# v split into hi and lo where it is projected, gated rows turned and split where they are made, and q read from PSUM in residue order

## The chip, the core and the metric

The kernel runs on one core of one Trainium2 chip. The metric is the device time of one execution in microseconds. A core has a matrix engine (PE, with its weight loads PEld), three engines that compute on tiles (DVE, ACT, POOL) and the engine SP, which here issues every DMA. Each engine runs its own instructions in order and waits on semaphores for the others. Tiles lie in SBUF (on-chip memory, 128 partitions); PE writes into PSUM, which has 8 banks of 128 x 512 float32.

## What is computed

One decoder layer on 1024 tokens of width 1024, all in float32. Cut to the part that the change touches:

```
a = rmsnorm(x);  q, k, v, u, z = split(a @ w_in)          # each 1024 x 512
attn = dilated_attention(q, k, v)                          # 8 heads of 64; windows with dilation 1, 4, 16
sgu  = gelu(u) * (w_spatial_causal @ layernorm(gelu(z)) + b_spatial)      # chunks of 128 tokens
mixed = concat(rmsnorm(attn), rmsnorm(sgu)) @ w_out
h = x + rmsnorm(mixed)
h = h + rmsnorm((silu(g) * up) @ w_down)                   # g, up = rmsnorm(h) @ w_gate_up
out = h + sigmoid(h @ w_pe_gate + b) * (p @ w_pe_proj)
```

A key counts for a query if its distance is in one of the windows; the merged softmax is computed as one softmax with the bias `c_bias`. For the later 512 queries the keys of the first 512 tokens that lie at a multiple of 4 are handled by themselves ("far"): queries and keys are taken in the order of their residue modulo 4.

## The kernel before, in words

**Precision.** A float32 product is made of three passes in the faster format `float32r`: each operand is split into a rounded part *hi* and a rest *lo* (`split`, line 430: an ACT copy and a DVE subtraction), and hi·hi, hi·lo and lo·hi are summed in PSUM (`mm3`). Large products use a Winograd scheme with seven partial products, numbered `q` = 1 to 7 (`in_products`, lines 708 to 728).

**Order.** The kernel is written as a graph of operations (`Graph`). `Graph.order` (lines 224 to 364) plays the whole program through at build time with a price for every operation (`price`) and puts out the instructions of each engine in the order in which they started in that play; an operation that stands earlier in the program goes first among those that are ready. The play assumes that a DMA lands 1.7 us after its bytes have passed at 330 GB/s (lines 326 to 328). At run time each engine keeps that order and waits. Tiles come from pools with a fixed number of places: 47 of 4 KB a partition (`M`), 14 of 2 KB (`S`), and the 8 PSUM banks (`P`).

**Stages, with the times of the profile.** Until about 83 us: x is normed, turned and split (`x_chain`), `v_out` (line 634) projects v for eight tiles of 128 tokens, copies each from PSUM to SBUF and stores it to DRAM (`vd`, line 637). Until 165 us: z and u are projected; as each tile of 128 tokens is complete, `z_norm` and `mix` (lines 684 to 704) make the gated rows and store them to `sgud`. From 149 to 223 us: the projections of q and k. `q_out` (line 763) scales q into hi and lo and stores it; at the end of partial product 4, for the later 512 tokens, it also makes a second copy in residue order: `turned`, two ACT copies with strided reads for each of four head pairs (lines 768 to 772).

From 224 to 486 us the attention runs, a head pair at a time: `first_half` (line 1143) for four pairs, then `second_half` (line 1158) for four. `unit` makes scores on PE, the bias and the row minimum on DVE (`softmax`, line 837), the exponential on ACT, turns the result with PE transposes, splits it and multiplies by v. `load_v` (line 1134) loads 512 rows of v of a pair, `v_halves` (line 1131) splits them (ACT and DVE) into a tile that holds hi and lo beside each other, and `first_half` stores that tile to `vcd`, from where `second_half` loads it back in residue order for `far_unit` (line 903).

Between the units PE is given fill work from generators: `gated` (line 973: load the gated rows, sum of squares on ACT, `rstd` over POOL, four PE transposes, split, product with w_out), `ple`, and the first two partial products of the FFN (`first_products`). From 486 us to the end: the rest of the FFN and the output.

Of the kernel before, what the change touches and what calls it, by code (L numbers as in the profile page):

```python
# [113 lines left out]
class Graph:  # L114
# [109 lines left out]
    def order(self):  # L224
# [78 lines left out]
        while left:  # L303
# [10 lines left out]
            for e in engines:  # L314
# [11 lines left out]
                if e == "sync":  # L326
                    dma = max(dma, now + 0.4) + o.bytes / 330e3
                    o.end = dma + 1.7
                    lanes = lanes[1:] + [o.end]
                    at[e] = max(at[e], lanes[0])  # L330
                else:
                    o.end = now + took
# [56 lines left out]
def hybrid_block(ctx: ExitStack, tc, a, out):  # L389
# [106 lines left out]
    def rstd_from(ssq, n, count):  # L496

        r, r2 = T1(n), T1(n)
        act(r, ssq, AF.Copy, scale=1.0 / count, bias=EPS)
        tt(r2, r, mhalf[:, :n], ALU.pow, "gpsimd")  # L500
        return r2
# [132 lines left out]
    def v_out(t, terms):  # L634
        v = SM()
        copy(v, gemm(PB(), [(A.tok(q, t, k), w[k]) for q, w in terms for k in range(4)]))
        load(vd[t * P : (t + 1) * P], v)

    vd, sgud = DR([S, AW]), DR([S, AW])
# [56 lines left out]

    def mix(t, z, u):
        ps = PB((P, 4, P))
        for g in range(4):
            pe("matmul", ps[:, g, :], wmT[:, g, :], z[:, g, :], start=True, stop=True)  # L700
        for g in range(4):
            ug = u[:, g * P : (g + 1) * P]
            dve("scalar_tensor_tensor", out=ug, in0=ps[:, g, :], scalar=bsp[:, g : g + 1], in1=ug, op0=ADD, op1=MUL)
        load(sgud[t * P : (t + 1) * P], u)
# [58 lines left out]
    def q_out(src, dsts):  # L763
        hl = M(F32R, (P, 2, 512))
        G.call("scalar", "mul", hl[:, 0], src, HD**-0.5)
        dve("scalar_tensor_tensor", out=hl[:, 1], in0=src, scalar=HD**-0.5, in1=hl[:, 0].f32(), op0=MUL, op1=SUB)
        load(dsts[0], hl.f32())
        if len(dsts) > 1:
            turned = M(F32R, (P, 2, 512))
            for j in range(2):  # L770
                copy(turned[:, j].split(P), hl[:, j].f32().then(lambda v: v.rearrange("p (s c) -> p c s", c=4)))
            load(dsts[1], turned.f32())
# [10 lines left out]
    for q, banks in in_products(0, AW, qk_mm, (1, 2, 6, 5, 3, 7, 4)):  # L783
        for i in range(4):
            dst = {1: q_part[i], 2: q_part[i], 6: k_part[i][:, 0], 3: k_part[i][:, 0], 5: k_part[i][:, 1],
                   7: k_part[i][:, 1], 4: None}[q]
            if q in (1, 6, 5):
                copy(dst, banks[i])
            elif q != 4:
                tt(dst, banks[i], dst)  # L790
            if q == 2:
                q_out(dst, [q_low[i]])
            if q == 4:
                q_out(banks[i], [q_high[i], q_far[i]])
            if q in (3, 7):
                k_out(dst, LO if q == 3 else HI, i)
# [10 lines left out]
    def stacked_q(src):  # L807
        both = M(F32R, (P, 2, 512))
        for x, rows_ in enumerate(HALVES):
            load(both[rows_].f32(), heads_of(src[:, x, :]))  # L810
        return both[:, 0], both[:, 1]

    def prepare_low(pr):
        q, k = stacked_q(q_low[pr]), [M(F32R, (P, 2, 512)) for _ in range(2)]
        for x in range(2):
            for rows_ in HALVES:
                load(k[x][rows_].f32(), heads_of(k_all[pr][:, x, LO]))
        qk[pr] = [(q[hh], k[0][:, hh], k[1][:, hh]) for hh in range(2)]

    def prepare_high(pr):  # L820
        q, qf, k = stacked_q(q_high[pr]), stacked_q(q_far[pr]), [[M(F32R) for _ in range(2)] for _ in range(2)]
        for hh in range(2):
            for x in range(2):
                for rows_ in HALVES:
                    load(k[hh][x][rows_].f32(), k_all[pr][HALVES[hh], x, :])
# [133 lines left out]
    def group_chain(v, junk):  # L959


        rstd = rstd_from(sumsq(v, junk), 1, AW)
        hl = M(F32R, (P, 2, 4, P))
        split(hl[:, 0], hl[:, 1], transposed(v, 4))
        return rstd, hl

# [167 lines left out]
    def load_v(pr, rs):  # L1134
        v = SM(F32, (P, 4, P))
        load(v, vd[rs, pr * P : (pr + 1) * P].then(lambda x: x.rearrange("(j p) c -> p j c", p=P)))
        return v
# [5 lines left out]
    def first_half(pr, fills, then):  # L1143
        v, b, vs, both = load_v(pr, slice(0, 512)), M(F32, (P, 2, 512)), [], M(F32R, (P, 8, P))
        load(b, a["c_bias"][2 * pr : 2 * pr + 2, :, :512].rearrange("h p c -> p h c"))
        for hh in range(2):
            vhl = both[:, 4 * hh : 4 * hh + 4, :]
# [10 lines left out]
    def second_half(pr, fills, then):  # L1158
        v, v3, vs, biases = load_v(pr, slice(512, S)), SM(F32R, (P, 2, P)), [], []
        for hh in range(2):  # L1160
            b, vhl = M()[:, :896], M(F32R, (P, 8, P))
# [5 lines left out]
            vs.append({3: v3[:, hh, :], "far": vhl[:, :4, :], **{j: vhl[:, j, :] for j in range(4, 8)}})  # L1167
# [174 lines left out]
```

## Time and profile before

| | |
|---|---|
| median of 3 runs | 1191.13 us (1191.04 to 1193.01) |
| the profiled execution | 1191.37 us, span of its instructions 1189.2 us |
| PE busy | 1170.6 us, 98% |
| DVE busy | 866.3 us, 73% |
| ACT busy | 580.4 us, 49% |
| POOL busy | 54.7 us, 5% |
| mean granted clock of PE | 0.993 |
| DMA | 208.78 MB, mean 176 GB/s, 55.1% of the 16 engines' time |

The busy time of PE counts overlapping passes once, and PE is called busy when it runs at its lower clock too; the granted clock tells that apart. The time that the profile shows beyond the span (1191.37 less 1189.2) is 2.2 us.

### The profile page before, as it was taken

Reading aid. Unit: us, or ns where it says so; the run is one execution under the profiler, and the core shown is the slowest. Engines: PE = TensorE matmul, PEld = TensorE weight load, DVE = VectorE, ACT = ScalarE, POOL = GpSimd, SP = SyncE. Lnnn points to the kernel's source line nnn. Section 1 sums busy time; section 2 is a strip of 40 time slices with the busy share of each in tenths; the row PEclk is TensorE's granted clock in tenths of the full one; section 3 lists DMA queues with packets and bytes.
Section 4 is the critical chain, followed back from the end, with each engine's and each line's share of the span. In section 5 each row is a group of like instructions: output and inputs, shape, how many; then the busy total and the mean of one; then the engine's idle time right before and its main releaser. Section 6 shows DMA issues by size and latency. Waiting matters only on the chain.

```text
span 1189.2 us, 16376 instructions
## 1 busy us (share of the span) xinstructions
PE 1170.6 (98%) x5633; PEld 977.4 (82%) x5633; DVE 866.3 (73%) x1699; ACT 580.4 (49%) x1304; POOL 54.7 (5%) x68
## 2 busy tenths in 40 slices
PE   8999999899999999999999999999999999999998
PEld 6887888788888888888888888888888888888887
DVE  7888895456566566799988888887668965469643
ACT  8664335688768566667223232232344445358121
POOL 3001000000021000120000000000000000002000
PEclk9999999899999899999999999999999999999999
DMA  8214046999752996468456665545297333653111
GB/s 301 74 69 142 36 153 206 312 280 336 236 178 77 255 249 187 130 207 288 151 168 192 190 192 174 187 155 177 97 350 278 98 98 102 232 179 142 45 45 54
DMA packets 161245, 208.78 MB, mean 176 GB/s; under 512 B 12477, under 2 KB 89609, under 8 KB 161162
## 3 DMA queue, kind: packets, MB, share of 16 engines
q1 hardware_dynamic: 161162, 207.74, 55.1%
q8 instruction: 44, 0.72, 0.3%
q14 instruction: 39, 0.32, 0.1%
HBM read 147.63 MB, written 60.06 MB: 175 GB/s over the span
## 4 chain that ended last, share of the span: by engine, by line
PE 88%; DMA 5%; DVE 3%; ACT 3%; issue 0%; SPq 0%; POOL 0%; DVEq 0%; ACTq 0%
PE p L383 88%; ACT m L383 2%; DVE s L383 2%; DMA s<-d 1%; DMA m<-in_w_gate_up 1%; DVE m L383 1%; DMA m<-d 1%; DMA d<-s 1%; DMA m<-in_w_in 1%; DVE t L383 1%; ACT s L383 0%; DMA m<-in_c_bias 0%; SPq L383 0%; POOL m L383 0%; ACT L383 0%
## 5 line engine op out<-in xcount | busy, mean ns | idle before, releaser
L383 PE MATMUL p<-m,m 128*128 128x512 f32 (+2 forms) x4620 | 1071.5, 389 | 4.8 <-DMA m<-d 1.6
L383 PEld LDWEIGHTS p<-m,m 128*128 128x128 f32 x4620 | 849.9, 189 | 173.4 <-DVE m L383 3.1
L383 DVE TENSOR_TENSOR m<-m,m 128x512 fp32r<-128x512 f32 (+2 forms) x465 | 312.3, 704 | 70.4 <-ACT m L383 64.8
L383 ACT CAST m<-m 128x512 fp32r<-128x512 f32 x371 | 221.0, 633 | 193.0 <-PE p L383 152.6
L383 DVE TENSOR_TENSOR s<-p,s 128x512 f32<-128x512 f32 (+4 forms) x222 | 142.8, 654 | 88.2 <-PE p L383 52.1
L383 ACT ACTIVATE s<-s 128x512 f32<-128x512 f32 (+1 forms) x71 | 44.2, 626 | 222.9 <-DVE s L383 169.2
L383 DVE TENSOR_TENSOR m<-p,m 128x256 fp32r<-128x256 f32 (+3 forms) x132 | 61.1, 490 | 36.1 <-PE p L383 21.9
L383 POOL TENSOR_TENSOR t<-t,c 128x1 f32<-128x1 f32 (+1 forms) x56 | 39.7, 715 | 1025.8 <-ACT t L383 848.6
L383 ACT COPY s<-p 128x512 f32<-128x512 f32 (+1 forms) x122 | 62.1, 519 | 48.4 <-PE p L383 47.1
L383 ACT CAST m<-s 128x256 fp32r<-128x256 f32 (+1 forms) x121 | 53.7, 480 | 30.1 <-PE p L383 14.8
L383 DVE TENSOR_TENSOR s<-s,s 128x512 f32<-128x512 f32 x88 | 60.6, 692 | 4.9 <-ACT s L383 0.7
L383 DVE TENSOR_TENSOR m<-s,m 128x256 fp32r<-128x256 f32 (+1 forms) x121 | 58.1, 508 | 6.5 <-ACT m L383 6.5
L383 PE MATMUL p<-c,m 128*128 128x128 f32 x328 | 50.6, 282 | 4.1 <-ACT m L383 4.1
L383 PEld LDWEIGHTS p<-c,m 128*128 128x128 f32 x328 | 40.6, 145 | 10.3 <-ACT m L383 5.1
L383 PE MATMUL p<-s,m 128*128 128x128 f32 (+1 forms) x256 | 44.9, 279 | 0.8 <-ACT s L383 0.8
L383 PE MATMUL p<-c,s 128*128 128x128 f32 (+2 forms) x249 | 42.7, 282 | 1.9 <-DVE s L383 1.9
L383 ACT COPY m<-p 128x512 f32<-128x512 f32 (+1 forms) x72 | 31.3, 452 | 27.1 <-PE p L383 26.2
L383 ACT ACTIVATE m<-m 128x1024 f32<-128x1024 f32 x32 | 34.1, 1067 | 20.2 <-DVE m L383 15.9
L383 PEld LDWEIGHTS p<-s,m 128*128 128x128 f32 x256 | 39.3, 192 | 5.4 <-ACT s L383 1.7
L383 PEld LDWEIGHTS p<-c,s 128*128 128x128 f32 (+2 forms) x249 | 32.3, 146 | 11.0 <-DVE s L383 3.9
L383 DVE CUSTOM_DVE_ANT_0 m<-p,m 128x384 f32<-128x384 f32 (+2 forms) x64 | 30.1, 500 | 12.4 <-PE p L383 12.4
L383 ACT ACTIVATE m<-m,t 128x384 f32<-128x384 f32 (+2 forms) x64 | 36.8, 580 | 4.1 <-DVE t L383 3.9
(58 smaller groups left out, 513.0 us busy)
## 6 DMA issues: line engine op xcount, KB each, us to landing
d<-s SPq DMA_DIRECT2D x149, 256.0 KB, 3.0
m<-d SPq DMA_DIRECT2D x51, 512.0 KB, 4.1
m<-in_w_gate_up SPq DMA_DIRECT2D x88, 256.0 KB, 4.1
m<-d SPq DMA_DIRECT2D x87, 256.0 KB, 7.1
s<-d SPq DMA_DIRECT2D x56, 256.0 KB, 4.1
d<-m SPq DMA_DIRECT2D x28, 512.0 KB, 4.8
m<-in_w_down SPq DMA_DIRECT2D x44, 256.0 KB, 6.0
m<-in_w_in SPq DMA_DIRECT2D x20, 512.0 KB, 4.2
```

The source lines that it names most:

```text
L383: getattr(getattr(nc, o.engine), o.what)(*[real(v) for v in o.args], **{k: real(v) for k, v in o.kw.items()})
```

## The change

Five things are done. (1) `v_out` splits v straight out of PSUM (ACT copy and DVE subtraction) into a 4 KB tile that holds hi and lo of each head beside each other, and stores it with four DMAs, one for each head pair, to four DRAM tensors. `v_halves`, `vcd` and its stores go; the halves load hi and lo as they are needed, in residue order too. (2) `group_chain` for the gated rows (sum of squares, rstd, four transposes, split) is called in `mix`; `sgud` holds the turned hi and lo, and `gated` only loads them. (3) The residue-ordered q is made by a second `q_out` that reads the PSUM bank with a stride, in the place of the two ACT copies. (4) The build-time play lets a DMA land 3.0 us after its bytes instead of 1.7. (5) For some loads it counts 1/0.8 of their bytes.

```diff
...
                 if e == "sync":
                     dma = max(dma, now + 0.4) + o.bytes / 330e3
-                    o.end = dma + 1.7
+                    o.end = dma + 3.0
...
-    def rstd_from(ssq, n, count):
+    def rstd_from(ssq, n, count, dst=None):
 
-        r, r2 = T1(n), T1(n)
+        r, r2 = T1(n), T1(n) if dst is None else dst
...
     def v_out(t, terms):
-        v = SM()
-        copy(v, gemm(PB(), [(A.tok(q, t, k), w[k]) for q, w in terms for k in range(4)]))
-        load(vd[t * P : (t + 1) * P], v)
-
-    vd, sgud = DR([S, AW]), DR([S, AW])
+        v = M(F32R, (P, H, 2, HD))
+        ps = gemm(PB(), [(A.tok(q, t, k), w[k]) for q, w in terms for k in range(4)]).split(HD)
+        split(v[:, :, 0, :], v[:, :, 1, :], ps)
+        for pr in range(4):
+            load(vd[pr][t * P : (t + 1) * P], v[:, 2 * pr : 2 * pr + 2].f32())
+
+    vd, sgud = [DR([S, 2, 2, HD]) for _ in range(4)], [DR([P, 2, 4, P]) for _ in range(NT)]
...
+    def group_chain(v, junk, dst=None):
+        rstd = rstd_from(sumsq(v, junk), 1, AW, dst)
+        hl = M(F32R, (P, 2, 4, P))
+        split(hl[:, 0], hl[:, 1], transposed(v, 4))
+        return rstd, hl
...
-        load(sgud[t * P : (t + 1) * P], u)
+        sgu_rstd[t], hl = group_chain(u, SM(), C([P, 8])[:, :1])
+        load(sgud[t], hl.f32())
...
-    def q_out(src, dsts):
+    def q_out(src, dst):
         hl = M(F32R, (P, 2, 512))
-        G.call("scalar", "mul", hl[:, 0], src, HD**-0.5)
-        dve("scalar_tensor_tensor", out=hl[:, 1], in0=src, scalar=HD**-0.5, in1=hl[:, 0].f32(), op0=MUL, op1=SUB)
-        load(dsts[0], hl.f32())
-        if len(dsts) > 1:
-            turned = M(F32R, (P, 2, 512))
-            for j in range(2):
-                copy(turned[:, j].split(P), hl[:, j].f32().then(lambda v: v.rearrange("p (s c) -> p c s", c=4)))
-            load(dsts[1], turned.f32())
+        hi, lo = (hl[:, x].split(P) if len(src.idx.shape) > 1 else hl[:, x] for x in range(2))
+        G.call("scalar", "mul", hi, src, HD**-0.5)
+        dve("scalar_tensor_tensor", out=lo, in0=src, scalar=HD**-0.5, in1=hi.f32(), op0=MUL, op1=SUB)
+        load(dst, hl.f32())
...
             if q == 4:
-                q_out(banks[i], [q_high[i], q_far[i]])
+                q_out(banks[i], q_high[i])
+                q_out(banks[i].split(P).then(lambda v: v.rearrange("p a b -> p (a b)")
+                                             .rearrange("p (s c) -> p c s", c=4)), q_far[i])
...
-            load(both[rows_].f32(), heads_of(src[:, x, :]))
+            load(both[rows_].f32(), heads_of(src[:, x, :]), 0.8)
...
-        v = SM()
-        load(v, sgud[t * P : (t + 1) * P])
-        part[t] = M()
-        rstd, hl = group_chain(v, part[t][:, LO])
+        part[t], hl = M(), M(F32R, (P, 2, 4, P))
+        load(hl.f32(), sgud[t])
         for nh, cs in enumerate((LO, HI)):
-            act(part[t][:, cs], gemm(PB(group="fill"), half_terms(hl, ws[nh])), AF.Copy, scale=rstd)
+            act(part[t][:, cs], gemm(PB(group="fill"), half_terms(hl, ws[nh])), AF.Copy, scale=sgu_rstd[t])
...
-    vcd = [[DR([512, P]) for _ in range(2)] for _ in range(4)]
-    def v_halves(dst, v, hh):
-        split(dst[:, :, 0:HD], dst[:, :, HD:], v[:, :, hh * HD : (hh + 1) * HD])
...
+    def load_v(dst, pr, rs, order, **sizes):
+        load(dst.f32(), vd[pr][rs].then(lambda u: u.rearrange(order, **sizes)), 0.8)
...
     def first_half(pr, fills, then):
-        v, b, vs, both = load_v(pr, slice(0, 512)), M(F32, (P, 2, 512)), [], M(F32R, (P, 8, P))
...
-            v_halves(vhl, v, hh)
-            load(vcd[pr][hh].then(lambda u: u.rearrange("(j p) d -> p j d", p=P)), vhl.f32())
-            vs.append({j: vhl[:, j, :] for j in range(4)})
+        load_v(v, pr, slice(0, 512), "(j p) h x d -> p j (h x d)", p=P)
+        vs = [{j: v[:, j, hh * P : (hh + 1) * P] for j in range(4)} for hh in range(2)]
...
     def second_half(pr, fills, then):
...
+        load_v(vc, pr, slice(0, 512), "(s c) h x d -> s c (h x d)", c=4)
+        load_v(v3, pr, slice(384, 512), "p h x d -> p (h x d)")
+        load_v(v4, pr, slice(512, S), "(j p) h x d -> p j (h x d)", p=P)
         for hh in range(2):
...
-            load(vhl[:, :4, :].f32(), vcd[pr][hh].then(lambda u: u.rearrange("(s c) d -> s c d", c=4)))
-            load(v3[:, hh, :].f32(), vcd[pr][hh][384:512])
-            v_halves(vhl[:, 4:, :], v, hh)
...
```

The loads of k in `prepare_low` and `prepare_high` get the same 0.8.

## Rows read from the trace of the kernel before

**Rows 1.** Stages as windows: us; busy PE, PEld, DVE, ACT, POOL (count); clock; DMA share; GB/s.

```profile
0.00:14.00 14.00, 9.66 (x26) 5.79 (x27) 7.60 (x15) 9.11 (x20) 2.60 (x7) 1.00 0.83 301
14.00:104.00 90.00, 89.30 (x420) 73.85 (x419) 81.42 (x183) 57.27 (x136) 12.68 (x13) 1.00 0.34 111
104.00:165.00 61.00, 61.00 (x302) 51.57 (x301) 51.65 (x131) 21.95 (x43) 4.14 (x4) 1.00 0.25 83
...
221.00:240.00 19.00, 15.17 (x73) 12.18 (x73) 10.69 (x40) 16.59 (x30) 0.00 (x0) 0.82 1.02 368
240.00:400.00 160.00, 158.53 (x936) 136.10 (x935) 99.56 (x275) 121.25 (x348) 13.95 (x19) 1.00 0.75 218
400.00:416.00 16.00, 14.36 (x78) 13.08 (x77) 10.77 (x43) 9.57 (x31) 0.00 (x0) 0.79 1.08 293
416.00:480.00 64.00, 61.98 (x368) 52.84 (x367) 40.76 (x124) 40.99 (x118) 0.00 (x0) 1.00 0.77 216
480.00:1184.00 704.00, 703.85 (x3191) 585.09 (x3190) 527.41 (x831) 275.60 (x530) 19.44 (x22) 1.00 0.50 165
```

**Rows 2.** Who PE waited for, whole span: us in total, times, longest.

```profile
PE p L383 <- DMA m<-d: 1.6, 1, 1.6
```

**Rows 3.** Windows of 5 us after 225 us, columns as in rows 1.

```profile
225.00:230.00 5.00, 3.97 (x24) 2.99 (x22) 3.71 (x13) 5.00 (x7) 0.00 (x0) 1.00 1.03 313
230.00:235.00 5.00, 2.20 (x8) 1.48 (x8) 2.27 (x14) 4.97 (x11) 0.00 (x0) 0.64 0.99 361
235.00:240.00 5.00, 5.00 (x21) 4.14 (x21) 2.77 (x9) 3.14 (x10) 0.00 (x0) 0.68 1.03 419
```

**Rows 4.** The chain of waits from 221 to 240: start, us, what.

```profile
221.49 0.61 ACT m L383
...
223.14 8.68 ACT m L383 x10
...
231.83 1.28 ACT L383
...
233.67 6.34 PE p L383 x22
```

**Rows 5.** ACT by form, 221 to 234: xcount, busy us, mean ns, idle before.

```profile
L383 ACT CAST m<-m 128x512 fp32r<-128x512 f32 x8 | 8.4, 1120 | 0.0
L383 ACT ACTIVATE m<-p 128x512 fp32r<-128x512 f32 x4 | 2.3, 590 | 6.8 <-PE p L383 6.8
```

**Rows 6.** DVE by form, 221 to 234.

```profile
L383 DVE SCALAR_TENSOR_TENSOR m<-p,m 128x512 fp32r<-128x512 f32 x4 | 2.7, 689 | 8.7 <-ACT m L383 8.7
L383 DVE CUSTOM_DVE_ANT_0 m<-p,m 128x256 f32<-128x256 f32 x4 | 1.7, 420 | 0.0
```

**Rows 7.** Timeline near 389: start, us, engine, instruction; a read of far's PSUM bank.

```profile
389.83 0.59 ACT L383 COPY s<-p 128x512 f32<-128x512 f32 x1
```

**Rows 8.** DVE by form, 14 to 104.

```profile
L383 DVE TENSOR_TENSOR m<-s,m 128x256 fp32r<-128x256 f32 x32 | 11.9, 418 | 0.8 <-ACT m L383 0.7
...
L383 DVE TENSOR_TENSOR s<-p,s 128x512 f32<-128x512 f32 x8 | 5.5, 690 | 3.7 <-PE p L383 2.4 <-ACT s L383 1.3
```

**Rows 9.** ACT by form, 14 to 104.

```profile
L383 ACT CAST m<-m 128x512 fp32r<-128x512 f32 x29 | 17.1, 648 | 5.6 <-PE p L383 2.7 <-DVE m L383 1.6 <-DVE s L383 1.2
...
L383 ACT CAST m<-s 128x256 fp32r<-128x256 f32 x32 | 11.3, 415 | 0.3 <-DVE s L383 0.3
```

**Rows 10.** Timeline, 21 to 22: the issue of one store of v.

```profile
21.70 0.33 SPq L383 DMA_DIRECT2D d<-s  x1
```

**Rows 11.** DMA from 221 to 400: queue, packets, MB, share; issues with us to landing.

```profile
q1 hardware_dynamic: 25394, 41.65, 77.5%
...
m<-d SPq DMA_DIRECT2D x53, 256.0 KB, 7.1
```

**Rows 12.** DMA from 400 to 480.

```profile
q1 hardware_dynamic: 17813, 18.42, 82.9%
```

**Rows 13.** Window late in the z and u stage, columns as in rows 1.

```profile
142.00:165.00 23.00, 23.00 (x119) 19.56 (x118) 21.19 (x73) 7.74 (x18) 4.14 (x4) 1.00 0.10 36
```

More of the change, by code (lines that the diff above doesn't have):

```diff
@@ L695, in z_norm @@
         tt(z, z, lnb.over(4), ADD)
+    def group_chain(v, junk, dst=None):
[3 more added lines that the diff above has]
+        return rstd, hl
+    sgu_rstd = {}
     def mix(t, z, u):
@@ L791, in hybrid_block @@
             if q == 2:
-                q_out(dst, [q_low[i]])
+                q_out(dst, q_low[i])
             if q == 4:
-                q_out(banks[i], [q_high[i], q_far[i]])
+                q_out(banks[i], q_high[i])
+                q_out(banks[i].split(P).then(lambda v: v.rearrange("p a b -> p (a b)")
+                                             .rearrange("p (s c) -> p c s", c=4)), q_far[i])
             if q in (3, 7):
@@ L816, in prepare_low @@
             for rows_ in HALVES:
-                load(k[x][rows_].f32(), heads_of(k_all[pr][:, x, LO]))
+                load(k[x][rows_].f32(), heads_of(k_all[pr][:, x, LO]), 0.8)
         qk[pr] = [(q[hh], k[0][:, hh], k[1][:, hh]) for hh in range(2)]
@@ L824, in prepare_high @@
                 for rows_ in HALVES:
-                    load(k[hh][x][rows_].f32(), k_all[pr][HALVES[hh], x, :])
+                    load(k[hh][x][rows_].f32(), k_all[pr][HALVES[hh], x, :], 0.8)
         qk[pr] = [(q[hh], *k[hh], qf[hh]) for hh in range(2)]
@@ L957, in hybrid_block @@
     gain = {}
[L959 to L965, printed above, removed]
     def half_terms(hl, wp):
@@ L1127, in feed @@
             n -= got
-    vcd = [[DR([512, P]) for _ in range(2)] for _ in range(4)]
-    def v_halves(dst, v, hh):
-        split(dst[:, :, 0:HD], dst[:, :, HD:], v[:, :, hh * HD : (hh + 1) * HD])
[L1134 to L1137, printed above, removed]
+    def load_v(dst, pr, rs, order, **sizes):
+        load(dst.f32(), vd[pr][rs].then(lambda u: u.rearrange(order, **sizes)), 0.8)
     def fed(fills, share):
@@ L1143, in first_half @@
     def first_half(pr, fills, then):
-        v, b, vs, both = load_v(pr, slice(0, 512)), M(F32, (P, 2, 512)), [], M(F32R, (P, 8, P))
+        v, b = M(F32R, (P, 4, 2 * P)), M(F32, (P, 2, 512))
         load(b, a["c_bias"][2 * pr : 2 * pr + 2, :, :512].rearrange("h p c -> p h c"))
-        for hh in range(2):
-            vhl = both[:, 4 * hh : 4 * hh + 4, :]
-            v_halves(vhl, v, hh)
-            load(vcd[pr][hh].then(lambda u: u.rearrange("(j p) d -> p j d", p=P)), vhl.f32())
-            vs.append({j: vhl[:, j, :] for j in range(4)})
+        load_v(v, pr, slice(0, 512), "(j p) h x d -> p j (h x d)", p=P)
+        vs = [{j: v[:, j, hh * P : (hh + 1) * P] for j in range(4)} for hh in range(2)]
         for step in (0, 1):
@@ L1158, in second_half @@
     def second_half(pr, fills, then):
-        v, v3, vs, biases = load_v(pr, slice(512, S)), SM(F32R, (P, 2, P)), [], []
+        vc, v3, v4, vs, biases = M(F32R, (P, 4, 2 * P)), SM(F32R)[:, : 2 * P], M(F32R, (P, 4, 2 * P)), [], []
+        load_v(vc, pr, slice(0, 512), "(s c) h x d -> s c (h x d)", c=4)
+        load_v(v3, pr, slice(384, 512), "p h x d -> p (h x d)")
+        load_v(v4, pr, slice(512, S), "(j p) h x d -> p j (h x d)", p=P)
         for hh in range(2):
-            b, vhl = M()[:, :896], M(F32R, (P, 8, P))
+            b, cs = M()[:, :896], slice(hh * P, (hh + 1) * P)
             load(b, a["c_bias"][2 * pr + hh])
-            load(vhl[:, :4, :].f32(), vcd[pr][hh].then(lambda u: u.rearrange("(s c) d -> s c d", c=4)))
-            load(v3[:, hh, :].f32(), vcd[pr][hh][384:512])
-            v_halves(vhl[:, 4:, :], v, hh)
             biases.append(b)
-            vs.append({3: v3[:, hh, :], "far": vhl[:, :4, :], **{j: vhl[:, j, :] for j in range(4, 8)}})
+            vs.append({3: v3[:, cs], "far": vc[:, :, cs], **{4 + j: v4[:, j, cs] for j in range(4)}})
         stats[pr], far[pr] = [T1(8) for _ in range(4)], SM(F32, (P, 4, P))
```

## The prediction

> **What bounds the kernel now.** The first view to read is the busy time by stage [rows 1]. PE is busy to the last hundredth from 104 to 165 us and for all but 0.15 of the 704 us after 480, so over most of the span the time is the sum of PE's passes. The change neither adds nor removes a matmul or a PE transpose (the 32 transposes of the gated rows only move), so this sum stays. What can move is the time in which PE stands still or runs at its lower clock. Standing still is window less PE busy in rows 1: 4.3 us before 14, 0.7 from 14 to 104, 3.8 from 221 to 240, 1.5 from 240 to 400, 1.6 from 400 to 416, 2.0 from 416 to 480; the rest of the 18.6 us between the span and PE's busy time, 4 us, lies at the end. The start (the first loads) and the end (the last output tile) hold nothing that is touched. The middle is 9.8 us.
>
> The clock column gives the second part. It is 0.82 from 221 to 240 and 0.79 from 400 to 416, right after PE stood still, and 1.00 in the other middle rows; of the levels 1.2 and 2.4 GHz that means half speed for part of the window. In the second place the loss is 0.21 x 16 = 3.4 us. In the first, 0.64 over 230 to 235 is 3.6 us at half speed and 0.68 over 235 to 240 is 3.2 us [rows 3]; PE resumed at 233.67 [rows 4], so 2.3 us of it fell into idleness, and (3.6 - 2.3 + 3.2) / 2 = 2.2 us were lost. So 9.8 + 2.2 + 3.4 = 15.4 us of the 1189.2 us span are all that a rearrangement could win. The list of PE's waits has one for a load of a DRAM tensor that the kernel itself wrote, 1.6 us [rows 2]; that is the stall after 400.
>
> **The longest stall, from the projections to the attention.** The chain of waits from 221 to 240 [rows 4] is ACT: from 221.49 almost without a gap to 231.8, a table load of 1.28, then the first exponential, and at 233.67 PE's first transpose of it. Eight of ACT's instructions are the strided copies for residue order, 1.12 us each, 8.4 us in all; the four scalings of q out of PSUM take 0.59 each [rows 5]. The exponentials come later in ACT's order. The change takes the eight copies away and adds four scalings on ACT and four subtractions on DVE, both reading PSUM with a stride of 16 bytes. No row shows that read. From below stand the unstrided forms, 0.59 and 0.69 [rows 5, 6]; from above the ratio of the strided copy in SBUF to an unstrided one, 1120 / 648 = 1.73 [rows 5, 9], so 1.02 and 1.19. I take the lower ends, because far's own copy reads its PSUM bank in steps of 512 bytes and takes 0.59 [rows 7]. A gain per instruction below the unstrided form has no ground in any row.
>
> The Trainium skill (SBUF — State Buffer, section on Door 1, the DMA port swizzle) says that SBUF is read in lines of 16 bytes and PSUM in lines of 8, and that each access which crosses into a new line pays, so a step of four float32 gains nothing from PSUM. For SBUF the trace agrees (1.12 against 0.65), for PSUM the 0.59 speaks against it; by that page the sum would come out some 2 us worse, which is the third rival.
>
> So ACT's work up to the table load is 8 x 0.59 = 4.7 us instead of 10.8, and it ends near 226.3. Next late is DVE: its first subtraction can start at 221.49 + 0.61 = 222.1, and 8 x 0.69 = 5.5 us put its last at 227.6, with the bias reads of the first scores (0.42 each [rows 6]) behind them, since the subtractions stand earlier in the program. The first exponential then starts near 228.3, 4.8 us earlier. Not all of that is won: PE used the stall for score passes (3.97 of the 5 us after 225 [rows 3]), and with DVE late it can only fill three score banks (line 1295) before it waits again. From 223.8, where the products end, to 228.9 I estimate two thirds of that pace, 2.7 us of work in 5.1, so 2.4 us of idleness remain of 3.8, and the drop of the clock may remain. Gain between 1.4 (idleness 2.4, same clock loss) and 6.0 us (all); I take 3.5. On the other side of this term nothing is added to ACT or PE.
>
> **v.** Out of the attention go 16 ACT casts and 16 DVE subtractions of 256 columns (0.415 and 0.418 [rows 8, 9]): 6.6 and 6.7 us, none on a bound engine. With them goes the chain store of `vcd`, landing, load. Into 14 to 104 us come eight subtractions out of PSUM of 0.69 [rows 8], 5.5 us; ACT's eight copies stay. DVE is busy for 81.4 of these 90 us [rows 1], so 8.6 are free, yet PE's one stall there, 0.7 us, already waits for DVE behind `z_norm`. Cost 0 to 3, taken 1.0. SP issues 24 more stores of v, 0.33 us each [rows 10], 8 us; they now wait for DVE instead of ACT, and the loads of w_in for z and u queue behind them; DMA is used to a third there, which hides the rest. v now takes a place of the 4 KB pool; no view shows how full that is, and where it runs short, loads of weights start later, within the same ends.
>
> **Gated rows.** Eight sums of squares, rstds, transposes and splits leave 165 to 370 and enter 104 to 170: 5.5 us for DVE. For the first four tiles DVE has room (61.0 - 51.7 = 9.3 us free from 104 to 165 [rows 1], 7.5 of them before 142). The last four (2.8 us) fall into 142 to 165, where DVE has 1.8 us free [rows 13] and PE lives on weights that DVE is splitting at the same time. Cost 0 (DVE ahead) to 2.8 (all of it), taken 1.0. The fill work gets simpler: one load, then products; its splits no longer compete in the attention.
>
> **DMA.** From 221 to 400 a packet took 0.775 x 179 x 16 / 25394 = 87 ns at 1640 bytes, from 400 to 480 60 ns at 1034 [rows 11, 12]; a line through both gives the estimates 36 ns for 512 bytes, 59 for 1 KB, 106 for 2, 200 for 4. A pair's first half goes from 1536 packets of 512 bytes to 512 of 1 KB: 3.4 to 1.9 us of all 16 engines. Its second half: 3.4 to 4.0. A gated tile: +0.75. Over the attention that is -6.0 + 2.3 + 6.0, about even, and DMA is no gain and no loss.
>
> **The play's landing time.** A load in the attention landed 7.1 us after issue [rows 11]; the play supposed about 2.5, and now 3.8. Work fed by loads is put later and other work before it. This reaches the stalls after 240: 1.5, then 1.6 + 3.4, then 2.0, in sum 8.5 us. Since the play's landing is still far too early, I count half: 0.7 + 2.5 + 1.0 = 4.2. The ends are 8.5 and, as every order is dealt anew and a new stall may come, a loss of 5.0, the size of the one after 400.
>
> **Sum.** -3.5 - 4.2 + 1.0 + 1.0 = -5.7 us. Against the profiled execution, 1191.37, that is 1185.7; the median lies 0.24 lower, so 1185.5.
>
> **Rivals.** (1) *The stall changes engine.* DVE keeps the transition at 2.4 us idle with the old clock loss (-1.4), the stalls after 240 stay as large, and the projections cost 2: 1191.7. For it speaks that DVE has no gap in its eight subtractions; against it that the dearest stall after 240 is for a load [rows 2]. (2) *DVE binds the projections* (slower). The 16 new subtractions are 11.0 us, and DVE's free time from 14 to 165 is 17.9, most of it early. If a third of that is usable, 5 us remain on the path; PE then stands still in one piece and the clock falls as it did after 400 (3.4 us). With the 3.5 us of the transition won, 1191.1 + 8.4 - 3.5 = 1196. It decides when PE waits for a split of weights for more than some 2 us between 142 and 180. For it speaks DVE's 21.2 of 23 us [rows 13]; against it that PE did not wait there at all before. (3) *The strided PSUM read costs as in SBUF*: DVE's last subtraction slips by 4 x 0.5 = 2.0 us and the forecast with it, 1187.5. (4) *All goes*: -6.0 - 8.5 and nothing lost, 1176.7; with 1 to 2 us of new stalls, 1178. That the change does not do what it says could only be in the landing time, if the new order leaves the stalls where they are; that is in rival 1.
>
> **How the numbers follow.** Chances: forecast 0.46, rival 1 0.17, rival 2 0.20, rival 3 0.07, rival 4 0.10. A difference of 0.2%, 2.4 us, is about what can be told from no change: faster is below 1188.7, slower above 1193.5. Forecast, rival 3 and rival 4 are faster: 0.63; rival 1 is the same: 0.17; rival 2 slower: 0.20. The forecast's own range is 1181.5 to 1188.5. To leave out no more than 2 in 10 the range takes in rivals 1, 3, most of 4 and the milder part of 2: 1178 to 1195.
>
> **What would show it.** In the changed profile: no 1.12 us casts near 222 to 232, four scalings more, and the first transpose of an exponential some 5 us nearer to the last product of q and k; a clock above 0.82 there. PE's list of waits without a load of v and without a wait of 1.6 us on `m<-d`. DVE near 23 of 23 us late in the z and u stage, with PE's wait for DVE there at most 2 us in sum. Wrong would be the forecast if PE waits for DVE by over 3 us before the attention, or if the lower clock appears in more places than two.

## The result, and the profile after

The changed kernel takes 1181.31 us (median of 4 runs, 1180.66 to 1183.19), the kernel before 1191.09 beside it: a ratio of 0.9921 with a 95% interval of 0.9900 to 0.9942. The forecast was 1185.5 with 1178 to 1195: sign and range held, the gain was 9.8 us where 5.7 was forecast. The profiled execution took 1180.66 us and its span is 1178.9, against 1189.2 before.

The first view is again the busy time by stage, of the changed kernel, in the windows of [rows 1] and with the same columns (us; busy PE, PEld, DVE, ACT, POOL with counts; granted clock; DMA share; GB/s):

```profile
0.00:14.00 14.00, 8.47 (x23) 5.18 (x24) 6.51 (x14) 8.21 (x18) 2.31 (x7) 1.00 0.84 297
14.00:104.00 90.00, 85.20 (x396) 69.50 (x395) 82.12 (x177) 57.37 (x134) 15.76 (x15) 1.00 0.37 124
104.00:165.00 61.00, 61.00 (x306) 51.04 (x305) 45.17 (x119) 28.53 (x65) 7.39 (x11) 1.00 0.35 113
221.00:240.00 19.00, 19.00 (x90) 15.81 (x90) 10.90 (x25) 10.08 (x20) 0.00 (x0) 1.00 1.01 276
240.00:400.00 160.00, 159.64 (x951) 138.30 (x950) 103.10 (x292) 116.54 (x332) 8.90 (x13) 1.00 0.85 262
400.00:416.00 16.00, 15.21 (x93) 12.86 (x92) 11.74 (x45) 10.82 (x34) 0.00 (x0) 1.00 1.08 305
416.00:480.00 64.00, 64.00 (x394) 55.26 (x393) 43.72 (x137) 43.07 (x125) 0.81 (x2) 1.00 0.74 213
```

Three things are to be seen against [rows 1]. From 221 to 240 PE is busy for 19.00 of 19 us at full clock, where it was 15.17 at 0.82. After 240 it stands still for 0.36 + 0.79 us where it was 1.5 + 1.6 + 2.0, and none of these windows shows a lower clock. And from 14 to 104, where nothing was to be won, it now stands still for 4.8 us instead of 0.7. The list of what PE waited for follows (us in total, times, longest), first over the whole span; the load of a DRAM tensor of the kernel's own [rows 2] is gone from it:

```profile
PE p L383 <- DVE s L383: 3.1, 2, 1.6
PE p L383 <- DVE m L383: 2.9, 2, 2.2
PE p L383 <- DMA m<-in_ln_pre_mix: 2.5, 1, 2.5
PE p L383 <- ACT m L383: 2.1, 3, 1.6
```

The waits for `DVE s` and for `in_ln_pre_mix` are those of the start, before 14 us. The list from 14 to 221 us says for whom PE waits in the projections:

```profile
PE p L383 <- DVE m L383: 2.9, 2, 2.2
PE p L383 <- ACT m L383: 1.8, 2, 1.6
```

The transition to the attention, in the changed kernel: first ACT's timeline from 230 to 240 (start, us, instruction, idle before it), then the strided PSUM reads by form on ACT and on DVE from 228 to 241 (count, busy us, mean ns, idle before).

```profile
231.49 3.91 ACT L383 ACTIVATE m<-p 128x512 fp32r<-128x512 f32 x7 [7.02 <-PE p L383]
236.00 0.60 ACT L383 ACTIVATE m<-p 128x512 fp32r<-128x512 f32 x1 [0.59 <-DVE m L383]
236.73 0.69 ACT L383 ACTIVATE m<-p,c 128x512 f32<-128x512 f32 x1
237.44 1.28 ACT L383 ACT_TABLE_LOAD   x1
238.73 0.40 ACT L383 ACTIVATE m<-m,t 128x128 f32<-128x128 f32 x1
```

```profile
L383 ACT ACTIVATE m<-p 128x512 fp32r<-128x512 f32 x8 | 4.4, 602 | 7.8 <-PE p L383 7.0 <-DVE m L383 0.6
```

```profile
L383 DVE SCALAR_TENSOR_TENSOR m<-p,m 128x512 fp32r<-128x512 f32 x8 | 5.1, 686 | 6.5 <-ACT m L383 6.5
```

Four of the eight in each row read PSUM in steps of 16 bytes, and the mean of all eight is 602 and 686 ns; the unstrided ones alone had 590 and 689 in the kernel before [rows 5, 6]. The eight casts of 1120 ns are gone. From the first scaling of q to the first exponential it is now 238.73 - 231.49 = 7.2 us, where it was 231.83 + 1.28 - 221.49 = 11.6 [rows 4]: 4.4 us less, where 4.8 was forecast.

### The profile page after: what moved, and what is told of

It reads as the page before. It is cut to its first block, busy times and chain, and to the rows that moved or that the text cites. A ratio compares the mean times of both kernels' runs of the same rounds, so it can differ in the third digit from the quotient of the medians.

```text
span 1178.9 us, 16341 instructions
## 1 busy us (share of the span) xinstructions
PE 1162.9 (99%) x5633; PEld 971.8 (82%) x5633; DVE 869.3 (74%) x1694; ACT 571.7 (48%) x1284; POOL 56.8 (5%) x69
## 4 chain that ended last, share of the span: by engine, by line
PE 96%; DVE 1%; DMA 1%; ACT 1%; issue 1%; POOL 0%; SPq 0%; DVEq 0%; ACTq 0%; POOLq 0%
PE p L383 96%; DMA m<-in_w_gate_up 1%; DVE m L383 1%; DVE s L383 1%; ACT m L383 1%; DMA m<-in_x 0%; ACT s L383 0%; POOL t L383 0%; DVE c L383 0%; SPq L383 0%; DVEq L383 0%; ACT t L383 0%; ACTq L383 0%; POOLq L383 0%
## 5 line engine op out<-in xcount | busy, mean ns | idle before, releaser
L383 ACT CAST m<-m 128x512 fp32r<-128x512 f32 x363 | 212.1, 622 | 186.0 <-PE p L383 139.1
L383 ACT ACTIVATE s<-s 128x512 f32<-128x512 f32 (+1 forms) x79 | 49.3, 627 | 236.4 <-DVE s L383 173.9
L383 DVE TENSOR_TENSOR m<-p,m 128x256 fp32r<-128x256 f32 (+3 forms) x140 | 66.7, 503 | 43.4 <-ACT m L383 23.4
L383 POOL TENSOR_TENSOR t<-t,c 128x1 f32<-128x1 f32 (+1 forms) x48 | 35.7, 749 | 968.2 <-ACT t L383 965.8
L383 ACT COPY s<-p 128x512 f32<-128x512 f32 (+1 forms) x114 | 57.2, 511 | 38.1 <-PE p L383 36.7
L383 ACT CAST m<-s 128x256 fp32r<-128x256 f32 (+1 forms) x105 | 47.7, 489 | 20.7 <-DVE s L383 10.4
L383 DVE TENSOR_TENSOR m<-s,m 128x256 fp32r<-128x256 f32 (+1 forms) x105 | 51.7, 523 | 4.8 <-ACT m L383 4.6
L383 PE MATMUL p<-c,s 128*128 128x128 f32 (+2 forms) x249 | 46.9, 282 | 4.0 <-DVE s L383 3.1
L383 ACT CAST m<-p 128x256 fp32r<-128x256 f32 (+1 forms) x88 | 38.4, 524 | 15.0 <-PE p L383 14.6
```

What stands on the lines that cost most here:

```text
L383: getattr(getattr(nc, o.engine), o.what)(*[real(v) for v in o.args], **{k: real(v) for k, v in o.kw.items()})
```

## The experiments

The first four kernels are the kernel before with one part of the change, the next four the change with one part undone, the rest go after what the eight left open. Each ratio is to runs of the kernel before that were made beside that kernel (medians from 1189.5 to 1191.1 us). Idleness and clock are from windows of 5 us of one profiled execution of each kernel: window less PE busy, and (1 - granted clock) x window, summed over the stretch, the clock over 0 to 480 us. Other executions of the same kernel can have another clock: the mean over a run went from 0.993 to 0.998 in the kernel before, from 0.992 to 1.000 in e8_no_gated and from 0.995 to 1.000 in e10_v_short.

| kernel | us | ratio to before (95%) | PE idle 0-15 | 15-165 | 165-250 | 250-480 | clock deficit |
|---|---|---|---|---|---|---|---|
| before | 1191.1 | | 4.3 | 0.7 | 3.8 | 5.1 | 6.8 |
| after | 1181.3 | 0.9921 (0.9900-0.9942) | 5.5 | 4.8 | 0.0 | 1.2 | 0 |
| e1_q_only | 1189.2 | 0.9999 (0.9988-1.0011) | 5.0 | 0.7 | 1.0 | 8.1 | 3.4 |
| e2_play_only | 1189.0 | 1.0004 (0.9992-1.0016) | 4.4 | 0.7 | 4.0 | 5.9 | 5.1 |
| e3_v_only | 1202.3 | 1.0110 (1.0092-1.0127) | 4.6 | 2.0 | 3.3 | 10.5 | 8.6 |
| e4_gated_only | 1188.6 | 0.9992 (0.9979-1.0005) | 4.7 | 0.7 | 3.2 | 5.5 | 5.1 |
| e5_no_q | 1187.0 | 0.9973 (0.9960-0.9986) | 5.1 | 4.8 | 3.2 | 0.6 | 1.7 |
| e6_no_play | 1199.3 | 1.0083 (1.0064-1.0102) | 5.1 | 2.0 | 0.0 | 15.1 | 6.8 |
| e7_no_v | 1175.0 | 0.9882 (0.9865-0.9899) | 4.9 | 0.7 | 0.0 | 0.7 | 0 |
| e8_no_gated | 1186.1 | 0.9972 (0.9958-0.9985) | 4.5 | 4.8 | 1.0 | 2.5 | 3.4 |
| e9_one_store | 1179.6 | 0.9915 (0.9902-0.9927) | 5.1 | 3.6 | 0.0 | 1.8 | 0 |
| e10_v_short | 1183.3 | 0.9939 (0.9925-0.9953) | 4.3 | 4.9 | 0.0 | 0.7 | 0 |
| e11_no_v_4us | 1175.9 | 0.9891 (0.9876-0.9905) | 5.0 | 0.7 | 0.0 | 1.4 | 0 |
| e12_small_places | 1182.3 | 0.9935 (0.9921-0.9948) | 5.2 | 4.8 | 0.0 | 2.3 | 0 |

### One part alone

**e1_q_only**: before with the second `q_out` out of PSUM.

```diff
-                q_out(banks[i], [q_high[i], q_far[i]])
+                q_out(banks[i], q_high[i])
+                q_out(banks[i].split(P).then(lambda v: v.rearrange("p a b -> p (a b)")
+                                             .rearrange("p (s c) -> p c s", c=4)), q_far[i])
...
```

> The kernel before with the third part of the change alone: residue-ordered q by a second scaling out of PSUM instead of two strided ACT copies. Theory A (the stall between projections and attention is ACT's eight strided copies): PE's idle time in the 20 us around the end of the projections falls from 3.8 to 0 to 2.4 us, the clock there rises above 0.82, and the time falls by 3.5 us, between 1.4 and 6.0. Theory B (the stall went because the gated rows' products stand ready as fill work): without them PE stays idle for 3 us or more there, and the time falls by less than 1.5 us. Both: the strided reads out of PSUM take 0.6 on ACT and 0.69 on DVE, or, by the third rival, 1.0 and 1.2.

Measured 0.9999. The local effect is there in full: the stall before the attention shrank from 3.8 us of idleness to 1.0 and the clock stayed up there. But the time did not move. Idleness after 250 grew by 3.0 us, with new stalls of 1.8 and 1.7 us, and by 0.7 at the start; that gives back most of the gain, and the columns do not show where the rest went. Windows of e1_q_only, columns as above:

```profile
230.00:235.00 5.00, 5.00 (x32) 4.25 (x29) 3.21 (x9) 4.11 (x15) 0.00 (x0) 1.00 1.00 384
...
250.00:255.00 5.00, 3.20 (x20) 2.47 (x19) 3.15 (x9) 3.08 (x8) 0.00 (x0) 1.00 1.03 228
280.00:285.00 5.00, 3.28 (x24) 2.63 (x23) 1.66 (x9) 2.57 (x8) 0.00 (x0) 1.00 0.91 320
```

The first row answers the 2.20 us at a clock of 0.64 in [rows 3]; the other two are stalls that the kernel before did not have there.

**e2_play_only**: before with the later landing and the 0.8 for k.

```diff
-                    o.end = dma + 1.7
+                    o.end = dma + 3.0
...
```

> The kernel before with the new landing time of the play alone (3.0 us instead of 1.7, and 0.8 for the loads of q and k). Theory A (work fed by loads is put later, so the stalls after 240 us shrink): idle time between 240 and 480 falls from 5.1 us to about 2.5, the drop of the clock near 405 goes, the time falls by 4.2 us (0 to 8.5); the stall at 225 to 234 stays. Theory C (the order is dealt anew and nothing more): stalls of the same total size turn up in other places, time within 2.4 us of before.

Measured 1.0004. The stall after 400 shrank from 1.6 us with a lower clock to 0.8 without one, and one of 2.8 us with a clock of 0.69 behind it came at 435. By itself the order is dealt anew and no better, as theory C has it.

**e3_v_only**: before with v split at its projection, kept in four DRAM tensors and loaded by the halves; the play stays at 1.7 us.

```diff
-        v = SM()
-        copy(v, gemm(PB(), [(A.tok(q, t, k), w[k]) for q, w in terms for k in range(4)]))
-        load(vd[t * P : (t + 1) * P], v)
+        v = M(F32R, (P, H, 2, HD))
+        ps = gemm(PB(), [(A.tok(q, t, k), w[k]) for q, w in terms for k in range(4)]).split(HD)
+        split(v[:, :, 0, :], v[:, :, 1, :], ps)
+        for pr in range(4):
+            load(vd[pr][t * P : (t + 1) * P], v[:, 2 * pr : 2 * pr + 2].f32())
...
```

> The kernel before with v split at its projection and stored hi and lo, alone. Theory A: the stalls of 2.2 and 2.4 us which the changed kernel shows between 45 and 65 us come from v (DVE's eight more subtractions and the 4 KB places): PE idle from 14 to 104 grows from 0.7 to 3 to 5 us here too; the waits for the store and load back of vcd go; the time rises by 1 to 4 us. Theory C (the landing time made those stalls): idle from 14 to 104 stays below 1.5 us and the time is within 2.4 us of before.

Measured 1.0110: 13 us slower. Most of the added idleness lies after 250 (10.5 us instead of 5.1), not in the projections (2.0 instead of 0.7), so neither theory holds: v costs the projections less here than in the change, and most of the loss is elsewhere. The chain of waits of e3_v_only around its longest stall (start, us, what) ends at a load of a weight that ACT is to split:

```profile
391.93 10.09 PE p L383 x58
402.02 9.67 DMA m<-in_w_gate_up
...
411.79 0.63 ACT m L383
412.42 0.04 issue
412.46 3.55 PE p L383 x10
```

The load took 9.67 us. In ACT's order the cast of this weight, which is for the fill work, stands in front of the next exponentials; the play had put it there as if the load would land some 3.3 us after issue (1.6 for 512 KB at 330 GB/s, and 1.7).

**e4_gated_only**: before with `group_chain` called in `mix` and the turned halves stored.

```diff
-        load(sgud[t * P : (t + 1) * P], u)
+        sgu_rstd[t], hl = group_chain(u, SM(), C([P, 8])[:, :1])
+        load(sgud[t], hl.f32())
...
```

> The kernel before with the gated rows turned and split when made, alone. Theory A (ACT's strided copies hold the first exponentials): the stall at 225 to 234 stays above 2.5 us idle with a clock drop, DVE is 22 to 23 of 23 us busy late in the z and u stage and PE loses up to 1 us there; time 0 to 1 us above before. Theory B (products of the gated rows fill the gap): PE idle near 225 to 234 falls below 1.5 us, the clock stays at 1.00, and the time falls by 4 us or more.

Measured 0.9992, no difference, as theory A has it. The projections did not pay: 0.7 us of idleness before 165 as before, although DVE is busy for 22.02 of the 23 us from 142 to 165.

The four ratios multiply to 1.0105, 12 us slower, and together the parts are 9.8 us faster. So no sum of parts can be right here; what each is worth has to be read with the others present.

### One part undone

**e5_no_q**: the change, with the two ACT copies back in the place of the strided PSUM reads (the lines of e1_q_only the other way round).

> The changed kernel with its third part undone: the strided ACT copies for residue order are back. Theory A (ACT's copies make the stall): PE idle at the end of the projections returns to 2.4 to 3.8 us with a lower clock, the time rises by 3.5 us (1.4 to 6.0). Theory B (the products of the gated rows fill the gap whatever ACT does): idle there stays below 1 us, the time rises by less than 1.5 us.

Measured 0.9973, some 6 us slower than the change (0.0052 x 1191). The stall is back where it was, behind ACT's copies: the last four of them take ACT from 237.63 to the table load at 241.79.

```profile
235.00:240.00 5.00, 5.00 (x26) 4.25 (x25) 1.89 (x8) 5.00 (x7) 0.00 (x0) 1.00 0.91 220
240.00:245.00 5.00, 1.80 (x9) 1.14 (x7) 1.28 (x4) 4.97 (x11) 0.00 (x0) 0.88 1.02 412
245.00:250.00 5.00, 5.00 (x27) 4.12 (x26) 1.60 (x6) 3.88 (x12) 0.00 (x0) 0.78 1.02 418
```

ACT is busy for 5.00 and 4.97 us and PE for 1.80 (windows of e5_no_q): 3.2 us of idleness and a lower clock, most of the loss that the change removed.

**e6_no_play**: the change with 1.7 us and without the 0.8.

> The changed kernel with the landing time of 1.7 us back and every rate at 1. Theory A: the stalls after 240 us come back to some 2 to 5 us idle with one drop of the clock, the time rises by 4.2 us (0 to 8.5); the stall at the end of the projections stays closed. Theory C: the stalls of 4.6 us between 45 and 65 us go or move instead, and the time is within 2.4 us or lower.

Measured 1.0083: undoing two numbers of the play costs 19 us, though alone they were worth nothing; the range of theory A ended at 8.5. The idleness before 165 even shrinks (2.0); from 250 to 480 it is 15.1 us with a clock deficit of 6.8. The largest piece, first as windows of e6_no_play, then in ACT's timeline:

```profile
285.00:290.00 5.00, 2.52 (x19) 2.08 (x17) 1.25 (x4) 1.18 (x4) 0.00 (x0) 1.00 1.06 306
290.00:295.00 5.00, 2.12 (x10) 2.13 (x11) 1.26 (x5) 2.55 (x8) 0.00 (x0) 0.68 1.02 357
```

```profile
292.45 0.86 ACT L383 COPY s<-p 128x256 f32<-128x256 f32 x2 [6.27 <-DMA d<-s]
```

An ACT copy out of PSUM waited 6.27 us for a *store*. Read with the kernel, the copy's 2 KB tile reuses the place from which the store reads, and the play took that store for landed. Behind it in ACT's order stood what PE needed next. PE stood still for 2.48 + 2.88 us and resumed at the lower clock.

**e7_no_v**: the change without its v part (`vcd`, `v_halves` and the 2 KB copy of v as before).

> The changed kernel with its first part undone: v stored as float32, split in the attention and stored and loaded back as hi and lo. Theory A (v's subtractions and places make the new stalls): idle from 14 to 104 falls from 4.8 to about 1 us; after 240 us 1 to 2 us of waits for v come back; the time falls by 1 to 3 us. Theory C (the stalls at 45 to 65 us are the landing time's): idle from 14 to 104 stays at 3 to 5 us and the time rises by 0 to 3 us.

Measured 0.9882 (1175.01 us, 1174.54 to 1177.28): the fastest of all, 4.6 us (0.0039 x 1191) faster than the change, and the two intervals do not meet. PE stands still for 0.7 us before 165 and 0.7 after 250, and for nothing at the transition (windows of e7_no_v):

```profile
14.00:104.00 90.00, 89.31 (x419) 73.89 (x418) 81.42 (x183) 57.19 (x137) 12.73 (x13) 1.00 0.31 105
...
221.00:240.00 19.00, 19.00 (x103) 16.17 (x102) 10.04 (x29) 12.80 (x31) 0.00 (x0) 1.00 1.03 372
240.00:400.00 160.00, 159.34 (x951) 137.42 (x950) 106.72 (x304) 118.81 (x335) 8.95 (x13) 1.00 0.87 256
```

Theory A is borne out in the projections. Its 1 to 2 us of waits for v after 240 did not come, and the gain is above its 1 to 3 us.

**e8_no_gated**: the change with the gated rows kept unturned, as before.

> The changed kernel with its second part undone: gated rows stored as float32, turned and split in the attention. Theory A: idle at the end of the projections stays at 0 to 2.4 us, the time falls or rises by less than 2 us. Theory B (their products are the fill work): PE idle returns there by 2 to 3 us with a drop of the clock, the time rises by 3 to 6 us.

Measured 0.9972, some 6 us slower than the change. In the profiled execution 1.0 us of idleness is at the transition and 1.3 more after 250. The rest is the clock after the stall of the projections, which is equally long in both kernels; the row after it is first from e8_no_gated, then from the change:

```profile
45.00:50.00 5.00, 2.82 (x13) 2.01 (x13) 5.00 (x13) 2.49 (x7) 0.00 (x0) 1.00 0.16 54
50.00:55.00 5.00, 5.00 (x15) 3.93 (x16) 4.97 (x13) 3.31 (x10) 0.26 (x1) 0.66 0.46 137
```

```profile
45.00:50.00 5.00, 2.82 (x13) 2.04 (x12) 5.00 (x14) 2.50 (x7) 0.00 (x0) 1.00 0.17 58
50.00:55.00 5.00, 5.00 (x23) 4.10 (x23) 4.97 (x13) 3.24 (x10) 0.33 (x1) 1.00 0.51 134
...
60.00:65.00 5.00, 2.60 (x13) 1.57 (x13) 4.18 (x10) 2.98 (x8) 0.00 (x0) 1.00 0.62 190
```

So 2.3 us of idleness speak for the gated part; whether the other 3 to 4 us belong to it is open. The runs with their clocks speak for a part of it: the eight of the twelve runs of e8_no_gated whose mean granted clock was 0.998 or more, as in all four runs of the change, took 1184.8 us on average (1182.1 to 1186.5), against 1181.6 (1180.7 to 1183.2). At a like clock that leaves some 3 us, near the 2.3. The other four runs, at 0.992 to 0.997, took 1186.8 to 1191.0; why their clock was lower is not shown.

### What v costs in the projections

The last fence above shows it for the change: two stalls, 2.18 us and 2.40, with DVE busy for 5.00 and 4.18 of the 5 us. By PE's timeline the first is a wait for DVE, the second one of 1.56 us for ACT and one of 0.75 for DVE. What precedes PE's z and u products is ACT's cast of their weights. From ACT's timeline, the first casts of 512 columns out of SBUF after 27 us (the group of three at the top is weights of v), first of e7_no_v, then of the change:

```profile
27.44 1.78 ACT L383 CAST m<-m 128x512 fp32r<-128x512 f32 x3
...
34.02 0.61 ACT L383 CAST m<-m 128x512 fp32r<-128x512 f32 x1
...
49.67 1.14 ACT L383 CAST m<-m 128x512 fp32r<-128x512 f32 x2 [1.12 <-PE p L383]
```

```profile
28.52 1.78 ACT L383 CAST m<-m 128x512 fp32r<-128x512 f32 x3
...
65.52 1.14 ACT L383 CAST m<-m 128x512 fp32r<-128x512 f32 x2 [1.30 <-PE p L383]
```

Without the v part three weights of z and u are split by 51 us, and PE multiplies z and u while v waits for its tokens; with it the first is split at 65.5, and PE has only v to do. Three kernels asked why.

**e9_one_store**: the change with one store of 512 KB per tile of v in the place of four.

```diff
-        for pr in range(4):
-            load(vd[pr][t * P : (t + 1) * P], v[:, 2 * pr : 2 * pr + 2].f32())
+        load(vd[t * P : (t + 1) * P], v.f32())
...
```

> The changed kernel with one store of v for each tile (512 KB, 4 KB runs, one DRAM tensor) instead of four of 128 KB; the loads read the same 1 KB runs. Theory D (the stalls of 2.2 and 2.4 us between 45 and 65 us come from the number of stores: with 3.0 us each in the play, four stores take four of its eight DMA lanes, so SP issues the weights of z and u later and PE runs out of work): idle from 14 to 104 falls from 4.8 to 1 us, the loads of w_in come near 22 us as before instead of 28, and the time falls by 4 to 5 us, near that of the kernel without the v part. Theory A (DVE's eight subtractions or the 4 KB places make them): idle stays at 3 to 5 us and the time is within 2 us of the changed kernel.

Measured 0.9915, as the change within the intervals; the idleness from 15 to 165 went from 4.8 to 3.6.

**e10_v_short**: the change with 1.7 us for the stores of v alone.

```diff
-                    o.end = dma + 3.0
+                    o.end = dma + (1.7 if getattr(o, 'short', False) else 3.0)
...
```

> The changed kernel in which the play counts 1.7 us of landing for the 32 stores of v alone and 3.0 for all else. Theory D (the landing time of these stores holds lanes or places of the play): the stalls between 45 and 65 us shrink from 4.6 to 1 to 2 us as in the runs with 1.7 for all, the stalls after 240 stay below 1.5 us, the time falls by 2 to 4 us. Theory A: idle from 14 to 104 stays at 3 to 5 us, time unchanged within 2 us.

Measured 0.9939, idleness 4.9: no better. The landing time of the stores in the play is not the cause, and their number accounts for at most 1.2 of the 4.8 us.

**e12_small_places**: the change with v split into two 2 KB tiles (16 splits of 256 columns) in the place of one of 4 KB, so that v no longer takes the places of the weights.

```diff
-        v = M(F32R, (P, H, 2, HD))
...
-        split(v[:, :, 0, :], v[:, :, 1, :], ps)
+        for i in range(2):
+            v = SM(F32R, (P, 4, 2, HD))
+            split(v[:, :, 0, :], v[:, :, 1, :], ps[:, 4 * i : 4 * i + 4, :])
...
```

> The changed kernel with v of a token tile in two tiles of 2 KB a partition (four heads each, from the other pool) instead of one of 4 KB; the same 32 stores to the same tensors, 16 splits of 256 columns instead of 8 of 512. Theory E (v's 4 KB tile crowds the pool from which the split weights of z and u come, so in the order their first products stand behind all of v, and PE has nothing to fill in with between 45 and 65 us): the split of these weights moves from 65 back to 35 to 52 us, idle from 40 to 70 falls from 4.8 to under 1.5 us, and the time falls by 3 to 5 us, to 1176 to 1178. Theory A (DVE's load of subtractions makes the stalls): DVE has 1.2 us more to do, idle there stays at 4 us or more, the time is the same or higher.

Measured 0.9935, no gain, but the profile moved as the theory of the places wants it up to a point. The z and u weights are split early again, at 37.08, and the idleness from 45 to 65 fell from 4.6 to 1.4 us. It came back as 3.1 us at 100 to 110, a wait for DVE like the first stall of the change; DVE is busy for 9.79 of those 10 us (cast and windows of e12_small_places):

```profile
37.08 1.14 ACT L383 CAST m<-m 128x512 fp32r<-128x512 f32 x2 [2.99 <-DMA m<-in_w_in]
```

```profile
45.00:65.00 20.00, 18.60 (x82) 14.40 (x81) 18.70 (x48) 11.62 (x34) 0.00 (x0) 1.00 0.40 119
100.00:110.00 10.00, 6.90 (x29) 5.03 (x28) 9.79 (x25) 1.94 (x5) 1.82 (x2) 1.00 0.06 9
```

The places decide where PE stands still (e12_small_places also halves the splits, which was not tried by itself). That it stands still for 4.8 us in either order fits a second limit, DVE's added subtractions; that the sum is the same in both is no proof of it, since the split of the two was not measured.

**e11_no_v_4us**: e7_no_v with 4.0 us in the place of 3.0, to see whether its time is one lucky order.

> The run without the v part (e7_no_v) with 4.0 us of landing instead of 3.0. Theory A (the play's landing is still too early against 7 us in the attention, so later is better): the idle left between 245 and 400, 0.7 us, does not grow and the time is 0 to 1 us lower. Theory C (each landing time deals another order, and 3.0 is one lucky deal): stalls of 2 to 10 us turn up somewhere, the time rises by 2 to 10 us.

Measured 0.9891 against 0.9882: the same. Two orders out of different landing times give the same time, which speaks against the luck of one deal; more than two were not tried.

## Why the prediction was right, and where it was not

**The balance.** From the table, before to after: +1.2 us of idleness at the start, +4.1 in the projections, -3.8 at the transition, -4.0 after 250. The clock gives 2.2 us at the transition and 3.4 after 400, as the prediction worked them out (the second is some 0.2 us too high: it counts about 0.3 us at the lower clock in which PE still stood, until 405.87). That is -8.1 of the -10.3 us of span. The other 2.2 are PE busy time that shrank beyond the clock (1170.6 to 1162.9 is 7.7, less 5.6) with the same 5633 matmuls and transposes; no view that was taken says where. Sign and range held, but hardly any term was near what it measured: two gained 2.5 and 3.2 us more than forecast, v cost about 3 to 5 more, and the gated rows changed sign. That the total came out within some 4 us of the forecast is in part luck, since these misses run against each other.

**The transition: right in mechanism, -6.0 for -3.5.** The strided copies on ACT were the cause (e1_q_only, e5_no_q), and the lower ends for the PSUM reads were the right choice: 602 and 686 ns. The mis-sized step is the estimate that 2.4 us of idleness would remain. e1_q_only leaves 1.0; the change leaves none, and e8_no_gated shows who closed it: without the gated part 1.0 us stays, with it the gated rows' products are ready as fill (the read of one at 236.73 in ACT's timeline). The prediction said of the gated part that "The fill work gets simpler" and gave that no figure.

The rule weighed there is that of the Trainium skill (SBUF — State Buffer, section on Door 1), of lines of 8 bytes in PSUM. The page puts its cost on matmuls; it was the prediction that carried it over to reads by ACT and DVE, as its third rival. For these two engines' reads the 602 and 686 ns decide against it.

**After 240: -7.4 for -4.2.** The gain was near its upper end of 8.5, and it was rightly ascribed to loads and stores that land later than the play supposes. What failed is the step that counted it as a term of its own. The landing time alone gains nothing (e2_play_only); with the other parts in the kernel it decides 19 us (e6_no_play). In the two stalls that were followed up, a place was reused after a store (e6_no_play) and a weight was cast ahead of the exponentials (e3_v_only); the other stalls of e6_no_play were not. The sizes show why 3.0 is nearer. These rows are of the changed kernel from 221 to 400 (count, KB each, median us from issue to landing), against the 7.1 of [rows 11]:

```profile
m<-d SPq DMA_DIRECT2D x51, 256.0 KB, 7.8
...
d<-s SPq DMA_DIRECT2D x20, 256.0 KB, 6.0
```

The play's 256 KB take 0.8 us at 330 GB/s and then 3.0. It is still too short, and 4.0 is no better (e11_no_v_4us), which suggests that what matters is not that the landing is right but that the order leaves some slack.

**v: +1.0 was forecast, it costs about 5.** This is the term that left its bounds of 0 to 3, on the slow side: 4.1 us of idleness in the projections (4.8 less 0.7). The prediction priced DVE's subtractions against DVE's free time, named the 4 KB pool as a risk and put it "within the same ends". There it failed: the order changes as a whole once v holds those places, the weights of z and u come some 31 us later (65.5 instead of 34.0), and PE stands still while waiting for DVE and ACT with no other product ready. By ratios v costs 4.6 us, by spans 1178.9 - 1173.0 = 5.9. And what it removes, ACT casts and DVE subtractions in the attention, was off the path, as said: without the v part PE stands still for 0.7 us after 250, with it for 1.2.

**Gated rows: +1.0 was forecast, it is a gain**, of some 3 us at a like clock (e8_no_gated), though nothing by itself (e4_gated_only). From 142 to 165 PE is busy throughout and DVE is *less* busy than in [rows 13], 17.59 instead of 21.19 us (the same window of the changed kernel):

```profile
142.00:165.00 23.00, 23.00 (x116) 18.92 (x115) 17.59 (x61) 11.60 (x29) 4.49 (x6) 1.00 0.31 114
```

The chains cost PE nothing there, even in e4_gated_only with DVE at 22.02 of 23 us.

**DMA: counted as about even.** In the prediction's count for the second half of a pair the packets are off: before, 1792 of 512 bytes (with the loads into `v3`), after, 1152 of 1 KB, so by its own line 4.0 to 4.3 us instead of 3.4 to 4.0, and +1 instead of +2.3 in all. The stores of v and of the gated rows were left out. Over the whole span the DMA engines were busy for 57.0% of 1178.9 us against 55.1% of 1189.2, some 17 us more. From 221 to 480 PE waits for no DMA in the changed kernel, so it is not seen to cost PE anything there.

**The signs.** The 1.12 us casts, the lower clock and the wait of 1.6 us on `m<-d` are gone, as it was put. DVE late in the z and u stage is not near 23 us but at 17.59. The sign of being wrong was PE waiting for DVE by over 3 us before the attention. From 14 to 221 us it is 2.9, just under; counted from the start, with 3.1 us more there (1.9 in the kernel before), it came, and the time was better than forecast all the same.

**The rivals.** The first (the stall changes engine) fell: PE waits for nobody at the transition, though e1_q_only by itself does end at no change, with the gain given back after 250. The slower one (DVE binds the projections) came true in part: PE does wait there for DVE, 2.9 us, but from 45 to 65 us, not from 142 to 180, and at full clock. The third fell with the 602 and 686 ns. The fourth, all goes, put "-6.0 - 8.5 and nothing lost" at 1176.7; the change without the v part comes to 1175.0, with idleness near nothing from 15 to 480 us.

**What stays open**: how the 4.1 us of v divide between places and DVE; the 2.2 us of PE busy time; the 1.2 us at the start, where the idleness varies from 4.3 to 5.5 us among the kernels of the table; how much of e8_no_gated's loss is the clock of its executions; whether e7_no_v needs the later landing, since q and gated together at 1.7 us were not tried.

## What to carry to other kernels

Where a planner deals the order anew, a local gain shows in the place where it was made and can be gone from the total: read the stage first, and judge a part by undoing it in the whole, not by adding it alone. When an early stage takes on work from a later one, look at the buffers it now holds and at who loses them, not only at the busy time of the engine that does it. A part that does what it was meant to do can still be the one to leave out: here the change without its v part beats both kernels.

## What the runs showed of the hardware that was not expected

A read of PSUM in steps of 16 bytes costs ACT and DVE next to nothing (602 and 686 ns for 128x512 as the mean of four strided and four plain reads, against 590 and 689 for plain ones), while a read of SBUF with that step took ACT 1120 ns [rows 5] against 648 for a plain one [rows 9].

The clock after a stall is not told by that stall's length alone. After 2.18 us of idleness at 45 to 50 us it stayed at 1.00 in the change and was 0.66 in e8_no_gated, with the rows before almost alike; 2.40 us at 60 to 65 us left it at 1.00 in the change; in the kernel before it fell within a wait of 1.64 us that ended at 405.87 [rows 1, 2]. These are single profiled executions; the mean clock of e8_no_gated went from 0.992 to 1.000 over its twelve runs, so the difference between the change and e8_no_gated need not come from the kernels.
